# Seven-product units: two of four weight sums made by transfers, the fold in smaller steps, and units in one pair fewer

## The chip, the cores and the metric

The kernel runs on one core of one Trainium2 chip. The metric is the device time of one execution in microseconds, as the median of several runs. A core has a matrix engine (TensorE, in the profile PE, with its weight loads as PEld), a vector engine (VectorE, DVE), an activation engine (ScalarE, ACT), a general engine (GpSimd, POOL) and an engine that here only issues transfers (SyncE, SP). They run side by side and wait for each other by semaphores. Transfers between DRAM and the on-chip memory run on 16 DMA engines; SP, ACT and POOL can issue them.

## The reference

Two layers of an encoder over 256 positions of width 2048 in float32: layer 0 mixes positions by grouped-query attention, layer 1 by dilated windows in three head groups. Each is followed by a gated MLP of width 5632 with a convolution over three positions. The change lies in that MLP's second half, the product with `w_down`:

```
def conv_ffn(h, w_up, conv_w, conv_b, w_down):
    u = h @ w_up                                  # 2048 -> 2 x 5632
    u = conv over 3 positions, per channel, + conv_b
    gate, val = jnp.split(u, 2, axis=-1)
    return (jax.nn.silu(gate) * val) @ w_down     # 5632 -> 2048

for i in range(DEPTH):                            # DEPTH = 2
    h = h + mixer(rms_norm(h, mix_norm[i]), ...)
    h = h + conv_ffn(rms_norm(h, ffn_norm[i]), w_up[i], conv_w[i], conv_b[i], w_down[i])
return rms_norm(h, final_norm)
```

## The kernel before, in words

**Products.** All float32 weights stream once from DRAM in tiles of 128 x 1024 (`raw`, 512 KB: two k-tiles of 128 rows by 512 columns). ACT rounds each into `wh`, DVE makes the rest `wl = raw - wh`, and the 256 positions (two halves m of 128) are kept as `xh`, `xl` in the same way. A product is three matmuls (`xh wh`, `xh wl`, `xl wh`), each 128 x 128 by 512 columns. `feed` (line 103) does this for one group kg of four k-tiles and one block n of 512 columns: two raw tiles, 24 matmuls. There are four raw tiles, two more in the MLP's down stage (`raw_tile`, line 97), and four each of `wh` and `wl`.

**The MLP.** `ffn` (line 368) treats the hidden width in two halves, six and then five pairs p of 512 gate and 512 value columns. Gate and value are evacuated, turned to channel-major by DVE transposes and 16 small copies (`turned`, line 421) into one of three buffers u0 to u2, run through the convolution (`conv`, line 405: four ACT operations, then eight on DVE), multiplied, and split again (`act_split`) to be the left side of the down product. The buffers go round: in a first half the last value uses u0, in a last half the last gate uses u0 and the last value u1. The last value's convolution (`flush`, line 580) runs while the down product has begun.

**Seven-product units.** In three of the four halves (layer 0's first, layer 1's both) the groups kg 2 and 3 go another way. Take the 256 positions as two halves, the four k-tiles as two halves and two blocks of columns n0, n1: that is a product of 2 x 2 blocks, and by a scheme of the Strassen kind it takes seven block products in place of eight, 42 matmuls where two `feed`s need 48. The left sides of the seven come from `combined` (line 476). On the right side four weight matrices b11, b12, b21, b22 are read, and four sums of them are formed by DVE in `fast_unit` (line 493): t1 = b11 + b12 (in u0), b12 + b22 (in place), t2 = b11 + (b12 + b22) (in u1), t4 = t2 + b21 (in u2). The products run in the order 1, 2, 3, 5 (t1), 7 (b12 + b22), 6 (t2), 4 (t4). Products 1, 5, 6 and 7 have four banks of their own; 2, 3 and 4 are added into the accumulators of the plain groups. `fold` (line 526) combines the four banks and adds them to h; it is a generator that is stepped beside the matmuls.

**Order.** `pair` (line 552) does two blocks of columns at once, with the groups and units in a written order. In a first half both pairs have units; in layer 1's last half too, and its last block ends in `project_last` (line 153), which finishes the two halves of the positions one after the other so that the first can be normalised and stored early. Generators in `pending` (evacuations, convolutions, splits) and in `beside` (the fold) are advanced by `step` at fixed places of `feed`: twice `pending`, twice `beside` for each. Before each unit `drain` advances them to their end. The order of issue on each engine follows the program's order with splits and sums drawn ahead (`high_priority`) and with buffers as they come free; each engine and each queue then works strictly in that order.

Of the kernel before, what the change touches and what calls it, by code (L numbers as in the profile page):

```python
# [13 lines left out]
P = 128  # L14
# [16 lines left out]
def tile_encoder(ctx: ExitStack, tc: tile.TileContext, x, xT, w_a, w_ao, q_gain, k_gain, w_b, w_bo,  # L31
# [70 lines left out]

    def feed(accs, lhs, kg, wap, first, last, by_m=False, pieces=1, mid=None, begun=()):
# [11 lines left out]
        def mms(order):  # L115
            for m, kt in order:
                (wh, wl), j = hls[kt // 2], kt % 2
                xh, xl = lhs[4 * kg + kt][:2]
                st, sp = first and kt == 0 and m not in begun, last and kt == 3
                c = slice(m * P, (m + 1) * P)  # L120
                nc.tensor.matmul(accs[m], xh[:, c], wh[:, j, :], start=st, stop=False)  # L121
                nc.tensor.matmul(accs[m], xh[:, c], wl[:, j, :], start=False, stop=False)  # L122
                nc.tensor.matmul(accs[m], xl[:, c], wh[:, j, :], start=False, stop=sp)  # L123
# [29 lines left out]
    def project_last(w, n, lhs, kgs, first_done, last_done):  # L153
# [16 lines left out]
        def mms(o, m, cols, kg, hls, first, last):  # L170
            for kt in range(4):
                (wh, wl), j = hls[kt // 2], kt % 2
                xh, xl = lhs[4 * kg + kt][:2]
                c = slice(m * P, (m + 1) * P)
                nc.tensor.matmul(o, xh[:, c], wh[:, j, cols], start=first and kt == 0, stop=False)
                nc.tensor.matmul(o, xh[:, c], wl[:, j, cols], start=False, stop=False)
                nc.tensor.matmul(o, xl[:, c], wh[:, j, cols], start=False, stop=last and kt == 3)
# [190 lines left out]
    def ffn(l, hT, ss_in, cw, g_next, last, side=None):  # L368
        with tc.tile_pool(name=nm("fpool"), bufs=1) as fp:
# [51 lines left out]
            def turned(s, u, by_act=0):  # L421
# [54 lines left out]
            def combined(cv, k0):  # L476
# [14 lines left out]
                return pick  # L491

            def fast_unit(acc, pick, wap0, wap1, begun, end):
                def load(wap, i):
                    r = raw_tile()
# [3 lines left out]
                def new_sum(i, x, y):  # L499
                    t = u_tile(i)[:, :1024].rearrange("p (a c) -> p a c", a=2)  # L500
                    nc.vector.tensor_tensor(t, x, y, ALU.add)  # L501
                    return t

                b11, b12, b21, b22 = load(wap0, 0), load(wap1, 0), load(wap0, 1), load(wap1, 1)
                with tc.high_priority(offset=2 * AHEAD):
                    t1 = new_sum(0, b11, b12)
                    nc.vector.tensor_tensor(b12, b12, b22, ALU.add)
                    t2 = new_sum(1, b11, b12)
                    t4 = new_sum(2, t2, b21)
                for i, (q, r) in enumerate(((1, b11), (2, b21), (3, b22), (5, t1), (7, b12), (6, t2), (4, t4))):  # L510
                    wh = spool.tile([P, 2, 512], F32R, tag="wh", name=nm("wh"), bufs=NHL)
                    wl = spool.tile([P, 2, 512], F32R, tag="wl", name=nm("wl"), bufs=NHL)
                    with tc.high_priority(offset=AHEAD):
                        nc.scalar.activation(wh, r, AF.Copy)  # L514
# [11 lines left out]
            def fold(acc, n0, n1):  # L526
# [13 lines left out]
                tt(hs(0, n0), hs(0, n0), a, ALU.add)  # L540
                tt(hs(0, n1), hs(0, n1), c, ALU.add)
                yield
                tt(hs(1, n0), hs(1, n0), w, ALU.subtract)
                tt(hs(1, n1), hs(1, n1), v, ALU.add)

            def fast_accs():
                (a3, a8), (a2, a4) = new_acc(), new_acc()
                acc = {q: ps_tile() for q in (1, 5, 6, 7)}
                acc.update({2: a2, 3: a3, 4: a4, 8: a8})
                return acc  # L550
# [774 lines left out]
```

## Time and profile before

| | |
|---|---|
| time, median of 3 runs | 2269.99 us (2268.06 to 2270.1) |
| the profiled execution | 2271.44 us, its span 2269.6 us |
| TensorE busy | 2237.2 us (99%), 10017 matmuls |
| VectorE busy | 1728.1 us (76%) |
| ScalarE busy | 1286.3 us (57%) |
| GpSimd busy | 717.4 us (32%) |
| moved by DMA | 439.57 MB, mean 194 GB/s |
| mean granted clock of TensorE | 0.996 |

Busy times are shares of the span of one profiled execution. A matmul's recorded time overlaps the next one's, so its cost is read from how many fit into a stretch. In a row of a group, `out<-in` names tiles, `xN` counts, and the numbers are busy us, mean ns of one, idle time before. A wait is put down to what ended last. Idle time of an engine that does not set the end costs nothing.

### The profile page before, as it was taken

What the parts mean: (1) busy time and instruction counts of PE and PEld (TensorE: products, weight loads), DVE (VectorE), ACT (ScalarE), POOL (GpSimd) and SP (SyncE); (2) the same over time, 40 slices, a digit from 0 to 9 for tenths busy, and PEclk for the clock granted to TensorE, in tenths of its full rate; (3) what the DMA queues carried; (4) which work ended last, traced back from release to release, by engine and by line L of the source; (5) the groups of instructions that cost most, each with busy time, mean ns of one, the idle gap of its engine ahead of it and who ended that gap; (6) DMA issues with size and microseconds to landing.
All of it is one profiled execution on the core that took longest, in us unless ns stands there. A gap on an engine that the chain in (4) does not pass through costs nothing.

```text
span 2269.6 us, 28639 instructions
## 1 busy us (share of the span) xinstructions
PE 2237.2 (99%) x10017; PEld 1848.8 (81%) x10017; DVE 1728.1 (76%) x2292; ACT 1286.3 (57%) x1791; POOL 717.4 (32%) x939
## 2 busy tenths in 40 slices
PE   9999999999999999999999999999999999999988
PEld 7888888887788888888888888888888878888866
DVE  6877867778866776878877886676768797677797
ACT  7575556556545656555454554445656655555654
POOL 3342065670005552010061007004656300365501
PEclk9999999999999999999999999999999999999999
DMA  8665655554565555565556545566655456555643
GB/s 302 194 219 181 214 195 192 195 194 163 202 205 192 192 195 193 177 206 195 190 187 189 191 168 186 182 202 200 204 194 192 171 204 202 192 194 193 199 169 132
DMA packets 126049, 439.57 MB, mean 194 GB/s; under 512 B 14280, under 2 KB 18120, under 8 KB 125904
## 3 DMA queue, kind: packets, MB, share of 16 engines
q1 hardware_dynamic: 123056, 429.05, 56.5%
q0 software_dynamic: 2560, 8.39, 1.6%
q8 instruction: 78, 1.28, 0.2%
q14 instruction: 67, 0.55, 0.1%
q10 hardware_dynamic: 288, 0.30, 0.0%
HBM read 432.34 MB, written 5.34 MB: 193 GB/s over the span
## 4 chain that ended last, share of the span: by engine, by line
PE 87%; DVE 5%; DMA 2%; POOL 2%; issue 2%; ACT 1%; SPq 0%; DVEq 0%; POOLq 0%; ACTq 0%
PE acc L122 27%; PE acc L121 27%; PE acc L123 27%; DMA raw<-in_w_down_dram 2%; POOL wide L269 2%; DVE wl L515 1%; DVE wl L134 1%; DVE u L501 1%; DMA raw<-in_w_a_dram 1%; PE ps L522 0%; PE ps L521 0%; PE ps L520 0%; PE ps L231 0%; DVE cv L416 0%; PE ps L230 0%
## 5 line engine op out<-in xcount | busy, mean ns | idle before, releaser
L134 DVE TENSOR_TENSOR wl<-raw,wh 128x1024 fp32r<-128x1024 f32 (+1 forms) x756 | 939.7, 1250 | 393.3 <-ACT wh L133 389.0
L133 ACT ACTIVATE wh<-raw 128x1024 fp32r<-128x1024 f32 (+1 forms) x756 | 790.5, 1050 | 680.7 <-PE acc L123 604.0
L121 PE MATMUL acc<-wh,xh 128*128 128x512 f32 x2176 | 848.3, 390 | 0.1
L122 PE MATMUL acc<-wl,xh 128*128 128x512 f32 x2176 | 847.4, 389 | 0.4 <-DVE wl L134 0.2
L123 PE MATMUL acc<-wh,xh 128*128 128x512 f32 x2176 | 847.2, 389 | 0.0
L429 POOL COPY u<-quad 32x256 f32<-32x256 f32 x640 | 457.3, 715 | 331.5 <-DVE quad L265 306.3
L123 PEld LDWEIGHTS acc<-wh,xh 128*128 128x128 f32 x2176 | 408.4, 188 | 85.1
L122 PEld LDWEIGHTS acc<-wl,xh 128*128 128x128 f32 x2176 | 408.7, 188 | 84.8 <-DVE wl L134 2.2
L121 PEld LDWEIGHTS acc<-wh,xh 128*128 128x128 f32 x2176 | 408.7, 188 | 84.0 <-ACT wh L133 0.5
L121 PE MATMUL acc<-wh,a 128*128 128x512 f32 x816 | 319.0, 393 | 7.2 <-DVE h L337 3.7
L122 PE MATMUL acc<-wl,a 128*128 128x512 f32 x816 | 319.9, 392 | 3.1 <-DVE wl L134 3.0
L123 PE MATMUL acc<-wh,a 128*128 128x512 f32 x816 | 319.2, 391 | 0.0
L121 PEld LDWEIGHTS acc<-wh,a 128*128 128x128 f32 x816 | 154.6, 189 | 40.6 <-ACT wh L133 4.5
L122 PEld LDWEIGHTS acc<-wl,a 128*128 128x128 f32 x816 | 154.2, 189 | 36.5 <-DVE wl L134 4.8
L123 PEld LDWEIGHTS acc<-wh,a 128*128 128x128 f32 x816 | 154.1, 189 | 32.3 <-DVE a L216 0.2
L269 POOL COPY wide<-quad 32x256 f32<-32x256 f32 x165 | 107.2, 650 | 171.8 <-DVE quad L265 162.7
L399 POOL MEMSET u<- 128x4 f32 x12 | 1.0, 106 | 421.0 <-DVE wl L515 233.3
L365 ACT ACTIVATE stg<-acc,rstd 128x512 f32<-128x512 f32 x122 | 82.7, 684 | 32.3 <-PE acc L123 32.3
L446 POOL TENSOR_TENSOR cv<-cg,cv 128x1024 f32<-128x1024 f32 x18 | 57.9, 3215 | 108.3 <-DVE cv L416 108.3
L416 DVE SCALAR_TENSOR_TENSOR cg<-u,cw,cg 128x256 f32<-128x256 f32 x176 | 81.7, 507 | 4.5 <-ACT cg L408 4.5
L514 ACT ACTIVATE wh<-raw 128x1024 fp32r<-128x1024 f32 x48 | 50.6, 1058 | 56.2 <-PE acc L123 47.2
L416 DVE SCALAR_TENSOR_TENSOR cv<-u,cw,cv 128x256 f32<-128x256 f32 x176 | 73.9, 477 | 2.9 <-ACT cv L408 2.8
(220 smaller groups left out, 1738.5 us busy)
## 6 DMA issues: line engine op xcount, KB each, us to landing
raw<-in_w_up_dram SPq DMA_DIRECT2D x352, 512.0 KB, 4.5
raw<-in_w_down_dram SPq DMA_DIRECT2D x176, 512.0 KB, 4.5
raw<-in_w_b_dram SPq DMA_DIRECT2D x144, 512.0 KB, 4.4
raw<-in_w_bo_dram SPq DMA_DIRECT2D x48, 512.0 KB, 3.7
raw<-in_w_a_dram SPq DMA_DIRECT2D x40, 512.0 KB, 4.7
raw<-in_w_ao_dram SPq DMA_DIRECT2D x32, 512.0 KB, 4.3
raw<-in_w_a_dram SPq DMA_DIRECT2D x16, 256.0 KB, 5.8
there<-quad POOLq DMA_DIRECT2D x6, 512.0 KB, 3.3
```

The source lines that it names most:

```text
L121: nc.tensor.matmul(accs[m], xh[:, c], wh[:, j, :], start=st, stop=False)
L122: nc.tensor.matmul(accs[m], xh[:, c], wl[:, j, :], start=False, stop=False)
L123: nc.tensor.matmul(accs[m], xl[:, c], wh[:, j, :], start=False, stop=sp)
L133: nc.scalar.activation(wh[:, c], r[:, c], AF.Copy)
L134: nc.vector.tensor_tensor(wl[:, c], r[:, c], wh[:, c].bitcast(F32), ALU.subtract)
L269: nc.gpsimd.tensor_copy(o[32 * c:32 * c + 32, :, 32 * q:32 * q + 32], quad[32 * q:32 * q + 32, c])
L365: nc.scalar.activation(o[:, m, :], accs[m], AF.Copy, scale=rstd[:, m:m + 1])
L416: nc.vector.scalar_tensor_tensor(cj, halves(flat[:, j, o:o + NT])[:, ::-1], tap(n, j, i), cj, ALU.mult, ALU.add)
L429: nc.gpsimd.tensor_copy(o, src)
L446: made.append(eng.tensor_tensor(cv, cg, cv, ALU.mult).ins)
L501: nc.vector.tensor_tensor(t, x, y, ALU.add)
L514: nc.scalar.activation(wh, r, AF.Copy)
```

## The change

In `fast_unit` two of the four sums are no longer made by DVE. t1 and t3 = b12 + b22 are made by loading the first matrix and then adding the second by an accumulating transfer that GpSimd issues; t1 goes into u0 and t3 into a raw tile. t2 = t1 + b22 and t4 = t2 + b21 stay on DVE and are issued at the product that needs them. A unit issues seven transfers instead of four. `fold` yields after nearly every operation. In `pair` the four extra banks are taken at the first unit, pending work is advanced by two more steps after each plain group in the first pair, and is brought to its end only before the first unit. The 16 copies of the last value alternate between GpSimd and ACT (all on ACT before). In layer 1's last half the second pair has no units: its two blocks are plain (`project`, `project_last`), for which `plain_too` keeps the left sides of groups 2 and 3 in plain form as well; `of_m` picks a half of the positions from either form. There are ten units instead of twelve.

```diff
+    def of_m(x, m):
+        return x[m] if isinstance(x, tuple) else x[:, m * P:(m + 1) * P]
...
-            def turned(s, u, by_act=0):
+            def turned(s, u, by_act=False):
...
-                    if i < 16 - by_act:
+                    if i % 2 == 0 or not by_act:
                         nc.gpsimd.tensor_copy(o, src)
...
-                turned(s, blk[1], 16 if blk[0] - NPAIR in (HALVES[0][1] - 1, NPAIR - 1) else 0)
+                turned(s, blk[1], blk[0] - NPAIR in (HALVES[0][1] - 1, NPAIR - 1))
...
-                    slots[-1 - k0 // 4] = combined(cv, k0)
+                    slots[-1 - k0 // 4], *rest = combined(cv, k0)
+                    if hf == 1:
+                        plain_too(k0, 20 + 2 * fast.index(k0 // 4), *rest)
...
+            def plain_too(k0, spot, v, sx):
+                c = pair_slot(spot, [P, 2, 2, P], F32R, "c")
+                split_in_order(c[:, 0], c[:, 1], v[:, 0, :, 1])
+                for kt in range(4):
+                    b, j = divmod(kt, 2)
+                    one = (sx[:, 4, j], sx[:, 5, j]) if b else (c[:, 0, j], c[:, 1, j])
+                    slots[k0 + kt] = (sx[:, b, j], one[0]), (sx[:, 2 + b, j], one[1])
...
-                b11, b12, b21, b22 = load(wap0, 0), load(wap1, 0), load(wap0, 1), load(wap1, 1)
-                with tc.high_priority(offset=2 * AHEAD):
-                    t1 = new_sum(0, b11, b12)
-                    nc.vector.tensor_tensor(b12, b12, b22, ALU.add)
-                    t2 = new_sum(1, b11, b12)
-                    t4 = new_sum(2, t2, b21)
-                for i, (q, r) in enumerate(((1, b11), (2, b21), (3, b22), (5, t1), (7, b12), (6, t2), (4, t4))):
+                def load_sum(wapx, i, wapy, k, r=None):
+                    r = load(wapx, i, r)
+                    nc.gpsimd.dma_start(r.rearrange("p a c -> p (a c)"), wapy[:, k * 1024:(k + 1) * 1024],
+                                        accum_op=ALU.add)
+                    return r
...
+                t1 = load_sum(wap0, 0, wap1, 0, spot(0))
+                b11 = load(wap0, 0)
+                t3 = load_sum(wap1, 0, wap1, 1)
+                b21, b22 = load(wap0, 1), load(wap1, 1)
+                t2, t4 = spot(1), spot(2)
+                for i, (q, r) in enumerate(((1, b11), (2, b21), (3, b22), (5, t1), (7, t3), (6, t2), (4, t4))):
...
                     with tc.high_priority(offset=AHEAD):
+                        if q == 6:
+                            nc.vector.tensor_tensor(t2, t1, b22, ALU.add)
+                        if q == 4:
+                            nc.vector.tensor_tensor(t4, t2, b21, ALU.add)
                         nc.scalar.activation(wh, r, AF.Copy)
                         nc.vector.tensor_tensor(wl, r, wh.bitcast(F32), ALU.subtract)
...
             def fold(acc, n0, n1):
...
                 nc.scalar.activation(a, acc[1], AF.Copy)
+                yield
                 tt(v, acc[6], a, ALU.subtract)
+                yield
                 tt(w, acc[7], v, ALU.add)
                 yield
...
-            def pair(wd, ns, lhs, order, done):
-                while beside:
-                    step(True)
-                acc, begun = fast_accs(), set()
+            def pair(wd, ns, lhs, order, done, hurry=False):
+                (a3, a8), (a2, a4) = new_acc(), new_acc()
+                acc, begun = {2: a2, 3: a3, 4: a4, 8: a8}, set()
...
-                    if side is None or kg == order[-1][0]:
-                        drain()
...
                     if side is None:
+                        if kg == fasts[0]:
+                            while pending or beside:
+                                step(True)
+                                if pending:
+                                    step()
+                            acc.update({q: ps_tile() for q in (1, 5, 6, 7)})
...
+                    for _ in range(2 * hurry):
+                        if pending:
+                            step()
                     if end:
+                        while beside and hf == 1:
+                            step(True)
                         done(sides[side], ns[side])
...
-                    pair(wd, (0, 1), slots, both[0] + both[1] + f0 + both[4] + f1 + both[5], done)
-                    pair(wd, (2, 3), slots, both[0] + f0 + both[1] + f1 + both[4] + both[5], done)
+                    for ns in (0, 1), (2, 3):
+                        pair(wd, ns, slots, both[0] + both[1] + f0 + both[4] + f1 + both[5], done, ns[0] == 0)
                     continue
-                pair(wd, (0, 1), slots, both[0] + [(1, 0)] + f0 + [(1, 1)] + f1 + both[4], done)
-                acc = pair(wd, (2, 3), slots, [(0, 0)] + f0 + [(1, 0)] + f1 + [(4, 0)], done)
-                while beside:
-                    step(True)
-                hs = h[:, 0, 1536:]
-                nc.vector.tensor_tensor(hs, acc[3], hs, ALU.add)
-                project_last(wd, 3, slots, rest, first_out, last_out)
+                pair(wd, (0, 1), slots, both[0] + [(1, 0)] + f0 + [(1, 1)] + f1 + both[4], done, True)
+                done(project(wd, 2, slots, list(range(np_))), 2)
+                project_last(wd, 3, slots, list(range(np_)), first_out, last_out)
```

More of the change, by code (lines that the diff above doesn't have):

```diff
@@ L119, in mms @@
                 st, sp = first and kt == 0 and m not in begun, last and kt == 3
[L120 to L123, printed above, removed]
+                xh, xl = of_m(xh, m), of_m(xl, m)
+                nc.tensor.matmul(accs[m], xh, wh[:, j, :], start=st, stop=False)
+                nc.tensor.matmul(accs[m], xh, wl[:, j, :], start=False, stop=False)
+                nc.tensor.matmul(accs[m], xl, wh[:, j, :], start=False, stop=sp)
         hls = []
@@ L173, in mms @@
                 xh, xl = lhs[4 * kg + kt][:2]
[L174 to L177, printed above, removed]
+                xh, xl = of_m(xh, m), of_m(xl, m)
+                nc.tensor.matmul(o, xh, wh[:, j, cols], start=first and kt == 0, stop=False)
+                nc.tensor.matmul(o, xh, wl[:, j, cols], start=False, stop=False)
+                nc.tensor.matmul(o, xl, wh[:, j, cols], start=False, stop=last and kt == 3)
         for i, (kg, hls) in enumerate(tail):
@@ L490, in combined @@
                     pick[q] = own[0][:, i], own[1][:, i]
-                return pick
+                return pick, v, sx
+            def plain_too(k0, spot, v, sx):
[5 more added lines that the diff above has]
+                    slots[k0 + kt] = (sx[:, b, j], one[0]), (sx[:, 2 + b, j], one[1])
@@ L493, in fast_unit, with load @@
             def fast_unit(acc, pick, wap0, wap1, begun, end):
-                def load(wap, i):
-                    r = raw_tile()
+                def load(wap, i, r=None):
+                    r = r or raw_tile()
                     nc.sync.dma_start(r.rearrange("p a c -> p (a c)"), wap[:, i * 1024:(i + 1) * 1024])
                     return r
[L499 to L502, printed above, removed]
```

13 lines of the change are left out of this document (6 added, 7 removed).

## The prediction

> **What bounds the kernel now.** I read the page's head first, then busy time by stretch, then the chain of waits on TensorE, then the timeline around the first seven-product unit. The head:
>
> ```profile
> span 2269.6 us, 28639 instructions
> PE 2237.2 (99%) x10017; PEld 1848.8 (81%) x10017; DVE 1728.1 (76%) x2292; ACT 1286.3 (57%) x1791; POOL 717.4 (32%) x939
> ```
>
> TensorE is busy 99% of the span, so only two things can move the time: matmuls added or taken away, and the gaps between them. The gaps lie in few places. Busy time by stretch (stretch, width, then busy us and count for PE, PEld, DVE, ACT, POOL, then granted clock, DMA share, GB/s); a plain stretch first, then the three places with units (A: first layer's first half; B: second layer's first half; C1 and C2: first and second pair of the last half):
>
> ```profile
> 2000.00:2100.00 100.00, 100.00 (x443) 82.81 (x442) 72.48 (x97) 59.83 (x77) 55.64 (x72) 1.00 0.58 192
> 540.00:600.00 60.00, 54.61 (x228) 43.12 (x227) 54.89 (x59) 27.90 (x31) 0.00 (x0) 0.97 0.54 184
> 1815.00:1865.00 50.00, 45.03 (x192) 35.47 (x192) 47.00 (x50) 26.79 (x29) 0.00 (x0) 1.00 0.61 209
> 2155.00:2185.00 30.00, 24.16 (x94) 18.15 (x93) 29.41 (x36) 17.93 (x26) 0.00 (x0) 0.94 0.42 143
> 2185.00:2230.00 45.00, 40.80 (x166) 32.42 (x165) 39.80 (x41) 23.92 (x28) 7.32 (x4) 0.92 0.49 167
> ```
>
> The plain stretch gives the price of a matmul: 100/443 = 0.226 us. TensorE's idle time (width less busy) is 5.4 in A, 5.0 in B, 5.8 in C1, 4.2 in C2. After a gap the granted clock falls, which costs about (1 - clock) x width: 1.8 in A, 0 in B, 1.8 in C1, 3.6 in C2. Losses: A 7.2, B 5.0, C1 7.6, C2 7.8, together **27.6 us**. That is all this change can win. DVE is 91 to 98% busy in A, B and C1 against 72% in the plain stretch. The waits on TensorE say the same:
>
> ```profile
> PE ps L521 <- DVE wl L515: 4.7, 4, 1.8
> PE acc L121 <- DVE h L337: 3.7, 2, 2.0
> PE ps L520 <- ACT wh L514: 3.6, 3, 2.3
> PE acc L121 <- DVE h L625: 3.5, 1, 3.5
> PE acc L122 <- DVE wl L134: 3.2, 4, 1.5
> PE acc L520 <- ACT wh L514: 1.2, 2, 0.6
> ```
>
> Lines 514 and 515 are the splits inside a unit; 337 and 625 are the residual adds between the two pairs (A, B; and C), which came late because DVE was at sums and folds. So DVE holds up TensorE here, directly or by sums that ACT waits for.
>
> **The change part by part.** DVE's and ACT's rows (count | busy, mean ns of one | idle before):
>
> ```profile
> L501 DVE TENSOR_TENSOR u<-raw,raw 128x1024 f32<-128x1024 f32 x24 | 29.3, 1221 | 7.8 <-DMA raw<-in_w_down_dram 7.6
> L507 DVE TENSOR_TENSOR raw<-raw,raw 128x1024 f32<-128x1024 f32 x12 | 14.7, 1222 | 2.7 <-DMA raw<-in_w_down_dram 2.7
> L501 DVE TENSOR_TENSOR u<-u,raw 128x1024 f32<-128x1024 f32 x12 | 14.6, 1218 | 0.0
> L515 DVE TENSOR_TENSOR wl<-raw,wh 128x1024 fp32r<-128x1024 f32 x48 | 58.1, 1220 | 9.9 <-ACT wh L514 9.9
> L514 ACT ACTIVATE wh<-u 128x1024 fp32r<-128x1024 f32 x36 | 38.1, 1060 | 34.0 <-DVE u L501 16.7 <-PE acc L123 13.9 <-PE acc L522 2.7
> L429 POOL COPY u<-quad 32x256 f32<-32x256 f32 x640 | 457.3, 715 | 331.5 <-DVE quad L265 306.3
> L431 ACT ACTIVATE u<-quad 32x256 f32<-32x256 f32 x64 | 26.8, 419 | 0.8
> ```
>
> *Sums.* There are 48 sums over 12 units, four each. A unit now costs DVE 4 + 7 operations x 1.22 = 13.4 us; with two sums left it costs 9 x 1.22 = 11.0. Its 42 matmuls, at the unit's own rate (541.48 to 545.67 is 18 of them, 0.233 each, rows below), take 9.8. DVE's debt per unit thus falls from 3.6 to 1.2 us. A plain group of weights lets DVE catch up: its 24 matmuls take 5.4 us and need two splits, 2.4 us.
>
> *Last half, second pair (C2).* Two units become plain work: 12 matmuls more, 12 x 0.226 = 2.7 us lost. In return no sum and no fold stands ahead of the residual add at line 625, and the new accumulators can take the pair of banks that is freed a group earlier. All 7.8 us should go, as plain stretches have no gap. Net gain **5.1**. The extra split for plain use of the two groups (one ACT and one DVE operation on 256 elements each, under half of 1.06 and 1.22 us) lies beside a plain group, where both engines have room; without that cover at most 2 x (0.53 + 0.61) = 2.3 us are lost.
>
> *Accumulating transfers.* The waits that this adds: SyncE's load of the first sum's base waits for buffer u0, which the convolution still reads; loads queued behind it wait too. POOL's accumulate then waits for that landing. Behind it on POOL stand only the second accumulate, and in C the multiplications by the final gain (7.32 us in C2's row), which nobody needs before the end. Transfers as the trace shows them (KB each, median us from issue to landing):
>
> ```profile
> raw<-in_w_down_dram SPq DMA_DIRECT2D x176, 512.0 KB, 4.5
> there<-quad POOLq DMA_DIRECT2D x6, 512.0 KB, 3.3
> oc<-in_onehot_dram POOLq DMA_DIRECT2D x1, 512.0 KB, 7.4
> ```
>
> No accumulate is in the trace. The lower bound is POOL's 512 KB store, 3.3; POOL's 512 KB load of 7.4 is the nearest row, the same size, queue and direction, so I take 7.4; it excludes nothing above, and I keep 14.8, twice it, as the upper end. A first sum is then ready for TensorE 4.5 + 7.4 + 1.06 (its ACT split) = 13.0 us after u0 is free.
>
> The Trainium skill ("Collectives: The Full Stack", section "The bandwidth ceiling: the fold count and why AG ≠ RS ≠ AR") says that an add in flight needs two source reads on the same read ring, so it moves at half the rate. No run here shows it. Only the moving part would double: an estimate from the row below, 0.524 MB at 345 GB/s, adds 1.5 us to each landing, and my sum would end at 2259 instead of 2256.
>
> Where does 13.0 us fit? Timelines of A and C (start, us, operation):
>
> ```profile
> 521.57 1.71 ACT L431 ACTIVATE u<-quad 32x256 f32<-32x256 f32 x4
> 540.26 1.40 DVE L416 SCALAR_TENSOR_TENSOR cv<-u,cw,cv 128x256 f32<-128x256 f32 x3
> 542.71 1.22 DVE L501 TENSOR_TENSOR u<-raw,raw 128x1024 f32<-128x1024 f32 x1
> 541.48 0.40 PE L520 MATMUL ps<-wh,sx 128*128 128x512 f32 x1
> 545.67 0.39 PE L520 MATMUL ps<-wh,s 128*128 128x512 f32 x1
> 547.39 0.50 PE L521 MATMUL ps<-wl,s 128*128 128x512 f32 x1 [1.34 <-DVE wl L515]
> ...
> 2144.66 0.48 DVE L416 SCALAR_TENSOR_TENSOR cg<-u,cw,cg 128x256 f32<-128x256 f32 x1
> 2164.01 1.40 DVE L416 SCALAR_TENSOR_TENSOR cv<-u,cw,cv 128x256 f32<-128x256 f32 x3
> 2165.44 1.23 DVE L501 TENSOR_TENSOR u<-raw,raw 128x1024 f32<-128x1024 f32 x1
> 2157.75 0.40 PE L520 MATMUL ps<-wh,sx 128*128 128x512 f32 x1
> 2161.94 0.39 PE L520 MATMUL ps<-wh,s 128*128 128x512 f32 x1
> 2167.87 0.50 PE L520 MATMUL ps<-wh,s 128*128 128x512 f32 x1 [2.31 <-ACT wh L514]
> 2170.13 0.50 PE L521 MATMUL ps<-wl,s 128*128 128x512 f32 x1 [1.75 <-DVE wl L515]
> ```
>
> In A, u0 is the last value's buffer: the last convolution ends at 541.66, and the unit's first sum starts right behind it. TensorE reaches the product of that sum (the fourth) at 545.67. The change frees u0 sooner: eight of sixteen copies leave ACT (8 x 0.42 = 3.4 us: 538.3 at the latest), and the steps are issued earlier. The floor is eight POOL copies from 521.57 at 0.72 (527.3) and a convolution that runs its course in some 6 us: 533.3. I take the middle, 535.8. The product is ready at 535.8 + 13.0 = 548.8, so TensorE waits 3.1 us, with 1.8 for the clock as in A now. A's other waits go: DVE has two sums fewer, and the fold no longer comes in a block before the add at 337. A: 7.2 to 4.9, gain **2.3**. B is built the same: 5.0 to 4.9, gain **0.1**. If the copies on POOL were slow and nothing came sooner, 541.66 + 13.0 - 545.67 = 9.0 would be waited, 5.9 more in each.
>
> In C1, u0 is the last gate's buffer, free at 2145.14, so its first product is ready at 2158.1, ahead of 2161.94. What TensorE waits for there now (2.31 and 1.75) is the third sum, whose buffer u1 the last convolution holds until 2165.41; 3.4 earlier is 2162.0, plus sum and split (1.22 + 1.06) 2164.3, when TensorE is at 2161.94 + 12 x 0.233 = 2164.7. The next unit's first sum: 2163.2 + 13.0 = 2176.2, needed at about 2157.75 + 60 x 0.233 + 24 x 0.226 = 2177.2. Both just fit; I leave 1.0 for DVE's debt. C1: 7.6 to 1.0, gain **6.6**. The later units of A and B have a full pair of groups (48 matmuls, 10.8 us) between them, and from one unit's third sum to the next one's fourth product TensorE has 12 x 0.233 + 10.8 + 18 x 0.233 = 17.8 us of work, against 13.0.
>
> *Transfers as a load.* A unit with its two groups reads 11 x 0.524 MB instead of 8 in 20.6 us: 280 GB/s instead of 204.
>
> ```profile
> 570.00:580.00 10.00, 10.00 (x45) 8.20 (x44) 10.00 (x11) 6.84 (x7) 0.00 (x0) 1.00 0.71 245
> ```
>
> Full queues would be 245/0.71 = 345 GB/s, so 280 is 81%. I cost it at nothing: buffers are loaded several groups ahead, and the first matrix's buffer now comes free right after its split. Views by index, the later allotment of four banks and the finer fold do no work of their own; DVE's fold operations stay, under plain groups.
>
> Sum: 2.3 + 0.1 + 6.6 + 5.1 = 14.1. The profiled execution took 2271.44 us (span 2269.6); 2257.3 is left, and the median of the runs stands 1.45 lower: **2256**.
>
> **Rivals.** *All waits go* (u0 at the floor 533.3, accumulates near 3.3): 27.6 - 2.7 = 24.9 gained, 2245. For it: 11.0 against 9.8 us is a small debt. Against it: the 7.4 row.
>
> *DVE still holds the units* (11.0 is above 9.8): A, B and C1 keep their 19.8, only C2's 5.1 is won: 2265. Against it: DVE's catch-up between units is 3.0 us a group.
>
> *Slower: accumulates that land late.* With landing time L, the waits are L - 4.3 in A and in B, L - 8.4 and L - 11.2 in C1's units; with 1.8 of clock at three places, 1.0 and 2.7, gain turns to loss at about L = 11.7. At 14.8 the sum is 40, 13 slower: 2283; and the other four units then lack 4.5 + 14.8 + 1.06 - 17.8 = 2.6 each: 2293. For it: no row of an accumulate, and a queue at 81%. Against it: L must exceed the nearest row by 4.3 us.
>
> **How the numbers follow.** My forecast (2251 to 2264) 0.48; all waits go 0.14; DVE still holds 0.12; late accumulates 0.22; something in between, such as loads stuck on SyncE behind the wait for u0, 0.04. About 0.2% (4.5 us) is what a measurement here tells from no change; half of the DVE case and the last one fall inside: faster 0.69, same 0.09, slower 0.22. The range 2245 to 2283 leaves out a few hundredths below and a tenth above.
>
> **What would show it.** Right: no gap after 2190 before the end; DVE's share in A and B near 80%; line 501's and 507's groups down to two sums a unit; the fourth product's split (ACT, from u0) waiting some 3 us for a POOL-issued transfer in A and B, not in C; that transfer landing near 7 us. Wrong: landings above 11 us, a DMA share near 0.9, waits of TensorE at plain loads behind a unit, or waits at the add on line 337's counterpart.

## The result, and the profile after

The changed kernel takes 2274.02 us (median of 20 runs, 2267.52 to 2282.83); the kernel before, run beside it, 2270.17 us. The ratio is 1.0018, with a 95% interval of 1.0009 to 1.0027: so some 4 us were lost where 14 were to be won. The profiled execution of the changed kernel took 2274.03 us with a span of 2272.2 us. Its head:

```profile
span 2272.2 us, 28705 instructions
PE 2241.3 (99%) x10029; PEld 1852.9 (82%) x10029; DVE 1688.0 (74%) x2251; ACT 1266.0 (56%) x1754; POOL 756.2 (33%) x991
```

There are the 12 more matmuls, and DVE is relieved of 40 us, as the change intends. The time is not shorter all the same. Busy time by stretch of the kernel after, with the two second pairs of the first halves added (600 to 640 and 1865 to 1915; columns as in the prediction):

```profile
540.00:600.00 60.00, 55.28 (x233) 44.32 (x232) 43.61 (x47) 28.69 (x30) 4.35 (x5) 0.97 0.79 240
600.00:640.00 40.00, 36.60 (x160) 29.42 (x159) 23.53 (x21) 18.87 (x19) 1.73 (x2) 1.00 0.74 211
1815.00:1865.00 50.00, 44.13 (x174) 34.53 (x173) 33.90 (x35) 22.97 (x23) 3.46 (x4) 0.90 0.77 218
1865.00:1915.00 50.00, 48.75 (x214) 39.61 (x213) 32.68 (x31) 23.68 (x23) 2.58 (x3) 1.00 0.76 233
2155.00:2185.00 30.00, 28.03 (x120) 21.88 (x119) 25.74 (x32) 20.50 (x30) 9.00 (x12) 1.00 0.78 215
2185.00:2230.00 45.00, 42.84 (x184) 33.83 (x183) 32.03 (x33) 22.72 (x28) 8.54 (x4) 1.00 0.74 233
```

The losses by the prediction's rule (width less busy, and (1 - clock) x width) give this table. Before, TensorE was busy 40.00 of 40 and 50.00 of 50 us in the two second pairs, so nothing was lost there.

| stretch | before | forecast | after |
|---|---|---|---|
| A, 540 to 600 | 7.2 | 4.9 | 4.7 + 1.8 = 6.5 |
| second pair behind A, 600 to 640 | 0 | 0 | 3.4 |
| B, 1815 to 1865 | 5.0 | 4.9 | 5.9 + 5.0 = 10.9 |
| second pair behind B, 1865 to 1915 | 0 | 0 | 1.25 |
| C1, 2155 to 2185 | 7.6 | 1.0 | 2.0 |
| C2, 2185 to 2230 | 7.8 | 0 | 2.2 |
| 12 more matmuls | - | 2.7 | 2.7 |
| sum | 27.6 | 13.5 | 28.9 |

So the last half came within 3.2 us of its forecast, and the two first halves, 12 us above theirs, took it all back. The waits on TensorE, after (engine, line waited for, us in total, times, longest):

```profile
PE ps L541 <- DVE wl L535: 9.0, 8, 2.8
PE ps L540 <- ACT wh L534: 5.8, 2, 3.4
PE acc L541 <- DVE wl L535: 3.3, 4, 1.5
```

The waits at the residual adds, 3.7 and 3.5 us before, are gone. What is left is at the splits inside the units (lines 534 and 535). Yet DVE, which makes those splits, was 91 and 94% busy in A and B before and is 73 and 68% busy now. It is late while it has time to spare. Its groups say why (count | busy, mean ns of one | idle time before them, and what ended it):

```profile
L531 DVE TENSOR_TENSOR u<-u,raw 128x1024 f32<-128x1024 f32 x10 | 12.3, 1226 | 56.8 <-DMA u<-in_w_down_dram 31.4 <-DMA raw<-in_w_down_dram 25.4
```

Line 531 is the third sum, t2 = t1 + b22. DVE stood still 56.8 us in front of its ten executions. In six of them (31.4 us) the accumulate that completes t1 (`u`) landed last; in the other four (25.4 us) it was the plain load of b22 (`raw`), the last of a unit's loads on SyncE. The timeline around the second unit of A shows what stands behind it. First DVE (start, us, operation, idle before), then TensorE at the unit's first two products, then the transfers issued from 545 to 570 (KB each, us from issue to landing) and the issue of the two that matter:

```profile
567.32 1.23 DVE L531 TENSOR_TENSOR u<-u,raw 128x1024 f32<-128x1024 f32 x1 [6.31 <-DMA u<-in_w_down_dram]
568.46 1.22 DVE L535 TENSOR_TENSOR wl<-raw,wh 128x1024 fp32r<-128x1024 f32 x1
569.60 1.22 DVE L533 TENSOR_TENSOR u<-u,raw 128x1024 f32<-128x1024 f32 x1
570.73 2.35 DVE L535 TENSOR_TENSOR wl<-raw,wh 128x1024 fp32r<-128x1024 f32 x2
...
568.39 0.40 PE L540 MATMUL ps<-wh,sx 128*128 128x512 f32 x1
569.73 0.50 PE L541 MATMUL ps<-wl,sx 128*128 128x512 f32 x1 [0.94 <-DVE wl L535]
572.00 0.50 PE L541 MATMUL acc<-wl,sx 128*128 128x512 f32 x1 [0.60 <-DVE wl L535]
...
u<-in_w_down_dram SPq DMA_DIRECT2D x1, 512.0 KB, 6.6
u<-in_w_down_dram POOLq DMA_DIRECT2D x1, 512.0 KB, 9.4
...
550.69 0.33 SPq L509 DMA_DIRECT2D u<-in_w_down_dram  x1
557.87 0.86 POOL L514 DMA_DIRECT2D u<-in_w_down_dram  x1 [14.23 <-DMA raw<-in_w_down_dram]
```

The unit's seven products are ordered so that the two sums made by transfers are wanted only at the fourth and fifth. But line 531, drawn ahead by its priority, stands in DVE's queue in front of the split (568.46) of the first product, which needs no sum at all. The base load is issued at 550.69, when u0 comes free, and lands 6.6 us later; the accumulate is issued at 557.87 (its row names a load beside it as the one that it waited for last) and lands 9.4 us later, at 567.3; only then may DVE go on. ACT had split the first matrix long before (560.43 to 561.49 on its timeline), so TensorE starts at 568.39 and stops at the second matmul.

### The profile page after: what moved, and what is told of

It reads as the page before. It is cut to its first block, busy times and chain, and to the rows that moved or that the text cites. A ratio compares the mean times of both kernels' runs of the same rounds, so it can differ in the third digit from the quotient of the medians.

```text
span 2272.2 us, 28705 instructions
## 1 busy us (share of the span) xinstructions
PE 2241.3 (99%) x10029; PEld 1852.9 (82%) x10029; DVE 1688.0 (74%) x2251; ACT 1266.0 (56%) x1754; POOL 756.2 (33%) x991
## 3 DMA queue, kind: packets, MB, share of 16 engines
q1 hardware_dynamic: 124496, 434.30, 58.2%
## 4 chain that ended last, share of the span: by engine, by line
PE 89%; DMA 4%; DVE 3%; POOL 2%; issue 1%; ACT 1%; SPq 0%; DVEq 0%; POOLq 0%; ACTq 0%
PE acc L125 28%; PE acc L124 28%; PE acc L126 28%; DMA u<-in_w_down_dram 2%; POOL wide L272 2%; DMA raw<-in_w_down_dram 1%; DVE wl L535 1%; DVE wl L137 1%; DMA raw<-in_w_a_dram 1%; PE ps L541 1%; PE ps L542 0%; PE acc L541 0%; PE ps L540 0%; ACT wh L136 0%; PE acc L542 0%
## 5 line engine op out<-in xcount | busy, mean ns | idle before, releaser
L137 DVE TENSOR_TENSOR wl<-raw,wh 128x1024 fp32r<-128x1024 f32 (+1 forms) x764 | 952.3, 1252 | 396.0 <-ACT wh L136 391.2
L136 ACT ACTIVATE wh<-raw 128x1024 fp32r<-128x1024 f32 (+1 forms) x764 | 799.5, 1050 | 707.0 <-PE acc L126 629.0
L432 POOL COPY u<-quad 32x256 f32<-32x256 f32 x672 | 477.3, 710 | 340.2 <-DVE quad L268 313.8
L534 ACT ACTIVATE wh<-raw 128x1024 fp32r<-128x1024 f32 x40 | 42.2, 1058 | 51.7 <-PE acc L126 23.5
```

The lines of the kernel that those rows point to most:

```text
L136: nc.scalar.activation(wh[:, c], r[:, c], AF.Copy)
L137: nc.vector.tensor_tensor(wl[:, c], r[:, c], wh[:, c].bitcast(F32), ALU.subtract)
L432: nc.gpsimd.tensor_copy(o, src)
```

## The experiments

The kernel before was run beside each group of four; the ratios are to it. Theory 1 was, at first, that the place of the sum t2 in DVE's queue takes the gain; theory 2 that the accumulates themselves are late or dear. From e9 on, the numbers of the theories belong to the single expectation.

**e1: each sum behind the split of the product before it.** `rest` is the DVE split of the last product.

```diff
                         if q == 6:
-                            nc.vector.tensor_tensor(t2, t1, b22, ALU.add)
+                            with tc.issue_after(rest):
+                                nc.vector.tensor_tensor(t2, t1, b22, ALU.add)
                         if q == 4:
-                            nc.vector.tensor_tensor(t4, t2, b21, ALU.add)
+                            with tc.issue_after(rest):
+                                nc.vector.tensor_tensor(t4, t2, b21, ALU.add)
...
-                        nc.vector.tensor_tensor(wl, r, wh.bitcast(F32), ALU.subtract)
+                        rest = nc.vector.tensor_tensor(wl, r, wh.bitcast(F32), ALU.subtract).ins
```

> One edit on the changed kernel: the third sum t2 (and t4) may stand on DVE only behind the split of the product before it, so it is no longer drawn ahead of the unit's first splits. Theory 1 (DVE's queue stands still behind a sum that waits for an accumulating transfer, and the first splits of the unit behind it are late): the waits at the first products of the later units go (some 5.6 us in the first layer's half, 5.5 in the second layer's, 2.7 in the last half), the wait at the fourth product of the first unit stays: about 2260. Theory 2 (the transfers themselves, queues at a share of 0.77 to 0.79): the waits stay whatever DVE's order, 2271 to 2275.

Measured: 2299.28 us, ratio 1.0122 (1.0108 to 1.0136), 25 us slower than the kernel after. Both theories missed it. Its waits:

```profile
PE ps L543 <- ACT wh L537: 9.6, 10, 2.4
PE ps L544 <- DVE wl L538: 8.4, 13, 0.8
PE acc L543 <- ACT wh L537: 8.0, 10, 0.9
```

The waits stand ten times or a little more, once in every unit: a split on DVE, then the sum, then its ACT split, then its DVE split, one behind the other. In its timeline the sum starts at 575.72 and the split of its result on DVE at 578.14, with 1.21 us idle between. Putting an operation as late as it can go leaves nothing to cover its own successors. So "behind" was right and "right behind" wrong.

**e2: t1 into a buffer that comes free sooner.** Before and after, t1 goes into u0, which in a first half the last convolution still reads when the first unit is near.

```diff
-                t1 = load_sum(wap0, 0, wap1, 0, spot(0))
+                at = (1, 2, 0) if hf == 0 else (2, 0, 1)
+                t1 = load_sum(wap0, 0, wap1, 0, spot(at[0]))
...
-                t2, t4 = spot(1), spot(2)
+                t2, t4 = spot(at[1]), spot(at[2])
```

> One edit on the changed kernel: t1 goes into the buffer that is free first (u1 in a first half, u2 in a last half) instead of u0, so that its load need not wait for the last convolution. Theory 1: the accumulate lands earlier, but the third sum is then drawn ahead of even the first unit's splits; little is won, 2268 to 2278. Theory 3 (the wait for u0 is what costs): the waits at the first unit's fourth product go, 5.2 us in the first layer and 6.6 in the second: about 2263.

Measured: 2269.35 us, ratio 0.9993 (0.9984 to 1.0002), 5 us better than after and in theory 1's range. The wait of the first units at the fourth product is gone, but the others grew:

```profile
PE ps L542 <- DVE wl L536: 14.0, 8, 4.5
```

At the second unit of A (DVE's row, and the accumulate's landing between 540 and 570):

```profile
565.02 1.23 DVE L532 TENSOR_TENSOR u<-u,raw 128x1024 f32<-128x1024 f32 x1 [8.74 <-DMA u<-in_w_down_dram]
u<-in_w_down_dram POOLq DMA_DIRECT2D x1, 512.0 KB, 11.8
```

t1's buffer is free at 546.2, 4.5 us sooner than in after, but TensorE, no longer held at the first unit, comes 5.8 us sooner too (562.59), and the accumulate now takes 11.8 us where it took 9.4. DVE stands still 8.74 us with the first splits behind it. One wait was traded for the other.

**e3: e1 and e2 together.** The diff is both.

> Both edits on the changed kernel: t1 in the buffer that is free first, and the sums behind the split of the product before. Theories 1 and 3 together: both kinds of waits go, 13.8 and some 11 us: about 2250. Theory 2: 2268 or more.

Measured: 2289.05 us, ratio 1.0079 (1.0066 to 1.0092). The new buffers make it 10 us better than e1, but it is far from the 2250 of theories 1 and 3: e1's chain stays (8.9 us in 11 waits for ACT's splits).

**e4: all four sums back on DVE, everything else of the change kept.** The two sums at the products 6 and 4 go.

```diff
-                t1 = load_sum(wap0, 0, wap1, 0, spot(0))
-                b11 = load(wap0, 0)
-                t3 = load_sum(wap1, 0, wap1, 1)
-                b21, b22 = load(wap0, 1), load(wap1, 1)
-                t2, t4 = spot(1), spot(2)
+                b11, t3, b21, b22 = load(wap0, 0), load(wap1, 0), load(wap0, 1), load(wap1, 1)
+                t1, t2, t4 = spot(0), spot(1), spot(2)
+                with tc.high_priority(offset=2 * AHEAD):
+                    nc.vector.tensor_tensor(t1, b11, t3, ALU.add)
+                    nc.vector.tensor_tensor(t3, t3, b22, ALU.add)
+                    nc.vector.tensor_tensor(t2, b11, t3, ALU.add)
+                    nc.vector.tensor_tensor(t4, t2, b21, ALU.add)
```

> The changed kernel with all four sums on DVE again, from four plain loads, as before; fold, steps, copies and the plain last pair stay changed. Theory 1: what the other edits win shows (5.1 us in the last pair, 3.7 and 1.8 at the residual adds between pairs), and DVE's debt at the first units stays: about 2260, so the accumulating transfers cost 14 us net. If the accumulating transfers help on the whole: above 2275.

Measured: 2256.18 us, ratio 0.9939 (0.9925 to 0.9952). This is the forecast's time, reached without the accumulating transfers that the forecast was about. Their part of the change, with the place that it gives t2 and t4, costs 1.0018 - 0.9939 = 0.79%, 18 us. Busy time by stretch in A and B of e4:

```profile
540.00:600.00 60.00, 59.71 (x261) 48.30 (x260) 53.19 (x55) 31.19 (x30) 0.00 (x0) 1.00 0.63 210
1815.00:1865.00 50.00, 49.82 (x219) 40.76 (x219) 41.22 (x42) 23.88 (x24) 0.00 (x0) 1.00 0.60 200
```

TensorE loses 0.3 and 0.2 us there, with DVE 89 and 82% busy and four sums in every unit. One wait of 1.3 us is left behind B, at 1877.56, and one in C1 that e9 looks at. So DVE can be that busy without holding TensorE up.

**e5: t2 and t4 behind the split of the third product.** This is the middle between after and e1: out of the first splits' way, with work left between the sum and the product that reads it. `made[q]` is the DVE split of product q.

```diff
                         if q == 6:
-                            nc.vector.tensor_tensor(t2, t1, b22, ALU.add)
+                            with tc.issue_after(made[3]):
+                                nc.vector.tensor_tensor(t2, t1, b22, ALU.add)
```

(and the same for t4).

> One edit on the changed kernel: t2 and t4 may stand on DVE only behind the split of the unit's third product, so neither ahead of the first splits nor (as in the run before) one by one between the last splits. Theory 1 (DVE's queue blocked by the early sum): the waits at the first products of the later units go, 13.8 us, and no chain of sum and split takes their place; the wait at the first units' fourth product stays: about 2260. Theory 2 (the transfers): 2271 to 2277.

Measured: 2267.18 us, ratio 0.9984 (0.9975 to 0.9993), 7 us better than after and between the two theories. The sum's group:

```profile
L533 DVE TENSOR_TENSOR u<-u,raw 128x1024 f32<-128x1024 f32 x10 | 12.2, 1221 | 14.1 <-DMA u<-in_w_down_dram 14.1
```

DVE stands still 14.1 us for it instead of 56.8, and at the first products TensorE waits no more. What stays, some 14 us in all, is the first units' wait for u0 (2.5 us the longest) and some 1 us a unit at the fourth product, where the two sums now stand in a row ahead of its split (570.83 and 572.09 in the second unit of A).

**e6: e5 and e2 together**, sums behind the third split and t1 in the buffer that is free sooner.

> The edit of the run before and t1 in the buffer that is free first. Theories 1 and 3: the first units' wait goes too, 5.2 and 6.6 us: about 2249, below the version with all sums on DVE (2256). If the transfers hold the units back as well: 2256 or more.

Measured: 2256.79 us, ratio 0.9933 (0.9919 to 0.9946). This is the time that the expectation gave for transfers that still hold the units back, not the 2249 of theories 1 and 3. DVE's idle time before t2 is 3.5 us in all, one wait for an accumulate in C1. TensorE still waits 7.1 us in seven places for DVE's splits, the longest of 2.0 us, at 2174.98, behind that one. So with queue and buffer mended the change as a whole wins 0.7%, but its accumulates win nothing over e4, whose DVE makes twice as many sums; and e9 below, which gives e4 the new buffers (and draws the last half's sums less far ahead), is 8 us faster than e6.

**e7: the addition left out of the transfers.** The same transfers in the same places, but without `accum_op`, so the second matrix overwrites the first and t1 and t3 are not sums.

> The changed kernel with the accumulating transfers as plain ones of the same size, issued by GpSimd at the same places with the same waits; left out of the computation is the addition (t1 and t3 are their second matrix alone). If the add in flight doubles a read and so delays the landing: from GpSimd's issue to landing falls from 8.8 us to 7.4 or less, and the time to 2265 to 2270. If the landing is that of GpSimd's queue under load: 8 us or more, and 2271 to 2277.

Measured: 2258.35 us, ratio 0.9939 (0.9927 to 0.9952), faster than either theory gave. So adding in flight alone costs 16 us here. t2 still stands in its bad place, and DVE still idles 42.4 us before it, but TensorE waits 8.5 us at the units' splits where it waited 18.9. The transfers from POOL, first after, then e7 (KB each, median us from issue to landing), and the queue they use (packets, MB, share of 16 engines' span), for both, with the plain queue of after:

```profile
raw<-in_w_down_dram POOLq DMA_DIRECT2D x10, 512.0 KB, 8.8
u<-in_w_down_dram POOLq DMA_DIRECT2D x10, 512.0 KB, 8.8
q1 hardware_dynamic: 124496, 434.30, 58.2%
q0 software_dynamic: 5440, 18.88, 4.2%
```

```profile
raw<-in_w_down_dram POOLq DMA_DIRECT2D x10, 512.0 KB, 6.7
u<-in_w_down_dram POOLq DMA_DIRECT2D x10, 512.0 KB, 7.3
q0 software_dynamic: 5440, 18.88, 3.0%
```

The landing is 1.5 to 2.1 us longer with the addition, as the first theory had it. For the same packets and bytes the queue takes 4.2% x 16 x 2272.2 = 1527 us of engine time against 3.0% x 16 x 2256.6 = 1083. The 444 us more, over 20 transfers of 512 KB in packets of 4 KB (2560), are 173 ns a packet (within 14, as the shares are rounded); a plain packet of q1 takes 58.2% x 16 x 2272.2 / 124496 = 170 ns. An accumulating packet costs about two plain ones.

That makes it a load on all other transfers too. These are the ten us in which the second unit of A is loaded and begins, first after, then e7 (columns as above):

```profile
560.00:570.00 10.00, 9.06 (x40) 7.22 (x39) 3.69 (x4) 4.25 (x4) 0.86 (x1) 1.00 0.97 254
560.00:570.00 10.00, 9.39 (x41) 7.35 (x41) 5.19 (x5) 4.68 (x6) 0.00 (x0) 1.00 0.71 282
```

With the addition the DMA engines are full (0.97) at 254 GB/s; without it 282 GB/s take a share of 0.71. How late an accumulate lands goes with that share. In after, t1's accumulate in the first units of A and B took 5.5 and 5.4 us, with shares of 0.52 and 0.58 between its issue and its landing (542.74 to 548.24, 1818.07 to 1823.45); those issued at 557.87 and 622.59 took 9.4 and 11.6, with 0.96 and 0.99.

**e8: the kernel before with only the second pair of the last half made plain** (`plain_too`, `of_m` and the two plain blocks; no accumulates, old fold, order and copies).

```diff
-                acc = pair(wd, (2, 3), slots, [(0, 0)] + f0 + [(1, 0)] + f1 + [(4, 0)], done)
...
-                project_last(wd, 3, slots, rest, first_out, last_out)
+                done(project(wd, 2, slots, list(range(np_))), 2)
+                project_last(wd, 3, slots, list(range(np_)), first_out, last_out)
```

> The kernel before with one part of the change alone: the last half's second pair without units. By the prediction's term for it 7.8 us of gaps go and 2.7 us of matmuls come: 5.1 us faster, 2266. Rival: the first pair's fold and residual adds now collide with the plain blocks, and nothing is won: 2271.

Measured: 2268.43 us, ratio 0.9993 (0.9984 to 1.0001).

```profile
2155.00:2185.00 30.00, 23.40 (x89) 17.70 (x88) 28.39 (x36) 17.55 (x25) 0.00 (x0) 0.89 0.33 114
2185.00:2230.00 45.00, 45.00 (x198) 36.84 (x198) 33.43 (x34) 24.28 (x29) 7.52 (x4) 1.00 0.65 226
```

C2 has no gap left, 7.8 us won for 2.7 us of matmuls, as forecast. C1 lost 2.3 us more than before (6.6 + 3.3 = 9.9 against 7.6), as the rival had it in part, which leaves 2.8. The medians differ by 2.4 us, but the interval still holds 1, so the gain itself isn't shown by the times.

**e9: e4 with the sums taken out of the way.** What was left in e4 was above all one wait of 4.29 us (behind it the granted clock was 0.50 from 2166 to 2170):

```profile
2163.74 1.22 DVE L527 TENSOR_TENSOR u<-u,raw 128x1024 f32<-128x1024 f32 x1
2164.87 1.22 DVE L137 TENSOR_TENSOR wl<-raw,wh 128x1024 fp32r<-128x1024 f32 x1
...
2166.15 0.80 PE L125 MATMUL acc<-wl,a 128*128 128x512 f32 x1 [4.29 <-DVE wl L137]
```

Here too sums (lines 524 to 527) stand ahead of a split that TensorE needs sooner, that of a plain group.

```diff
-                t1, t2, t4 = spot(0), spot(1), spot(2)
-                with tc.high_priority(offset=2 * AHEAD):
+                t1, t2, t4 = (spot(i) for i in ((1, 2, 0) if hf == 0 else (2, 0, 1)))
+                with tc.high_priority(offset=(2 - hf) * AHEAD):
```

> All four sums on DVE as in e4, the first sum now written to a buffer that is free before the last convolution ends (u1 in the first half, u2 in the last), and in the last half the sums are drawn ahead by 60 instead of 120 places. Theory 1 (what is left in e4 is the wait of the plain split in the second layer's first pair, 4.45 us at 2166.15 with the slower clock behind it, 2.5, and 2.5 us of first-unit waits, because the sums stand ahead of that split): these go, 2248 to 2252. Theory 2 (DVE's debt is simply moved to the split behind): 2255 or more.

Measured: 2249.01 us, ratio 0.9906 (0.9891 to 0.9921), 21 us faster than before and 25 faster than the change. Which of the two edits, the buffer or the later drawing in the last half, won how much of the 7 us over e4 was not asked. The 4.29 us wait is gone and no wait inside a unit is above 0.7 us:

```profile
PE acc L538 <- ACT wh L532: 0.7, 1, 0.7
```

It is the fastest kernel of this study, and beats both.

**e10, e11, e12: one more part of the change undone in e4 each**, to see which of them won A and B: the fold in four lumps (e10), all sixteen copies of the last value on ACT (e11), the old order of the second pairs (e12).

```diff
 # e11
-                    if i % 2 == 0 or not by_act:
+                    if not by_act:
 # e12
-                        pair(wd, ns, slots, both[0] + both[1] + f0 + both[4] + f1 + both[5], done, ns[0] == 0)
+                        pair(wd, ns, slots, (both[0] + both[1] + f0 + both[4] + f1 + both[5] if ns[0] == 0 else
+                             both[0] + f0 + both[1] + f1 + both[4] + both[5]), done, ns[0] == 0)
```

In e10 `fold` is as in the kernel before.

> e4 with the fold in four lumps as before, everything else of e4 kept. Theory 1 (the fold in single steps carries most of what the kept parts win in the first pairs, about 12 us): 2262 to 2268. Theory 2 (the earlier steps, the alternating copies or the order of the second pair carry it): 2255 to 2259.

> e4 with all sixteen copies of the last value on ACT as before. Theory 1 (sharing the copies with POOL frees u0 up to 3.4 us sooner and so starts the sums sooner): 3 to 7 us slower than e4, 2259 to 2263. Theory 2 (the copies were never late): 2255 to 2258.

> e4 with the second pair of the first halves in its old order (unit, two groups, unit, four groups). Theory 1 (the order of the second pair puts the units where DVE has caught up, and the add of the first pair no longer meets the first unit): waits come back at the second pairs of both first halves, 2 to 4 us each, 2260 to 2264. Theory 2 (the order does nothing): 2255 to 2258.

Measured: e10 2254.59 us, 0.9929 (0.9917 to 0.9942); e11 2261.11 us, 0.9958 (0.9946 to 0.9970); e12 2255.05 us, 0.9927 (0.9915 to 0.9940). Against e4's 0.9939, e10 and e12 are no slower, so the fine fold and the order win nothing by themselves. The copies seem to: 0.0019, some 4 us, when POOL takes half of them, though the intervals of e4 and e11 touch. The trace of e11 bears it out: its first sum in A starts at 540.38, e4's at 535.30, and more waits stand at the units' splits (e4 has 2.9 us in 4 in the first of these rows, none in the second):

```profile
PE ps L539 <- DVE wl L533: 4.3, 6, 1.7
PE acc L539 <- DVE wl L533: 3.6, 5, 1.1
```

Of e4's 14 us the copies hold about 4 and the plain second pair perhaps 2. The other 8 belong to what wasn't undone singly (the two extra steps after each plain group, work brought to its end only before the first unit, the four banks taken later) or to parts that need each other; which of these it is stays open.

## Why the prediction was wrong

The forecast was 2256 us and faster; 2274 us came. By its steps:

- *The bound and the sum to be won.* Right. Gaps were the only thing to win besides 12 matmuls, and e9 won 21 us, with those 12 matmuls in it.
- *Last half, second pair.* Right: no unit, no gap, and no wait at the add on line 625's counterpart. The 2.2 us that the table shows in C2 are the first pair's second unit (waits of 1.46 and 0.61 us at 2190.30 and 2192.57).
- *C1.* Half right: of 7.6 us 1.0 were to stay. 2.0 were lost before 2185, and with the second unit's two waits 4.1 in all. The forecast had that unit's first sum ready at 2176.2, 1 us before its use. Its accumulate was issued at 2179.35, and DVE waited for it until 2187.89 with the third product's split behind: the same failure as in the later units below.
- *The first units of A and B.* The wait for u0 came at the place forecast, 3.1 us with 1.8 of clock behind it. In A it was 2.42 and 0.76 us with 1.8 of clock; in B 3.40 and 0.47, and some 3.5 of the 5.0 of clock (0.92 and 0.73 in the two stretches of 10 us from 1815), so 2.5 more than forecast. That A fits so well is in part luck: u0 came free at 536.9 in place of 535.8 and the base took 5.3 us in place of 4.5, but the accumulate 5.5 in place of 7.4. TensorE, after:

```profile
549.46 0.51 PE L540 MATMUL ps<-wh,s 128*128 128x512 f32 x1 [2.42 <-ACT wh L534]
550.72 0.79 PE L541 MATMUL ps<-wl,s 128*128 128x512 f32 x1 [0.76 <-DVE wl L535]
...
636.59 0.50 PE L541 MATMUL ps<-wl,sx 128*128 128x512 f32 x1 [2.79 <-DVE wl L535]
...
1824.66 0.79 PE L540 MATMUL ps<-wh,s 128*128 128x512 f32 x1 [3.40 <-ACT wh L534]
1846.63 0.50 PE L541 MATMUL ps<-wl,sx 128*128 128x512 f32 x1 [2.00 <-DVE wl L535]
```

- *The later units of A and B: this step failed.* The forecast set 17.8 us of TensorE's work, up to the next unit's fourth product, against a chain of 13.0, so no wait. The rows at 569.73, 572.00, 636.59 and 1846.63 are such waits. With smaller ones and the slower clock the later units lost some 9.7 of the 12 us by which the first halves missed their forecast. Two things were wrong in the step.

  The first is the deadline. The step asked when TensorE reads t1, and not what is queued on DVE behind the sum that reads t1. With t2 in front of the first product's split, in the second unit of A the accumulate has to be there a sum and a split (2.4 us) before TensorE's second matmul at 568.6, so at 566.2: 15.5 us after u0 came free (550.67, the end of DVE's split of t1). Without t2 there, t1 would be wanted only for the split of the fourth product, which TensorE would reach at 568.39 + 18 x 0.233 = 572.6.

  The second is the size. The chain was put at 4.5 + 7.4 = 11.9 us to the landing; it took 550.67 to 567.3 = 16.6, the base 6.6 and the accumulate 9.4. With the forecast's 11.9 us even the bad place would have been harmless; with 16.6 it is 1.1 us late here, and TensorE's gap is 0.94. In the second unit of B it was not t1 that came last but b22's plain load, issued at 1833.16, 11.0 us from issue to landing where the median of such loads is 4.8. DVE's row, and the loads issued from 1833.1 to 1833.3:

```profile
1844.22 1.23 DVE L531 TENSOR_TENSOR u<-u,raw 128x1024 f32<-128x1024 f32 x1 [8.23 <-DMA raw<-in_w_down_dram]
raw<-in_w_down_dram SPq DMA_DIRECT2D x1, 512.0 KB, 11.0
```

  That both place and size count is what e5 (place mended, 7 us better) and e7 (addition left out, 16 us better) show.
- *Transfers as a load: mis-sized.* The forecast found a share of 81% for 280 GB/s and costed it at nothing. Over the whole of A the share was 0.79, but at 240 GB/s, and in the stretches where the later units' sums were loaded it was 0.97 (560 to 570 and 1835 to 1845). The sum counted an accumulate as one transfer; by e7 its packets cost two. An estimate with the two of a unit's and its groups' eleven transfers counted twice is 280 x 13/11 = 331 of the forecast's 345 GB/s, 96%. The loads into u0 from SyncE took 5.9 us (median) where 4.5 was taken, and plain loads from POOL take 6.7 to 7.3 (e7). That was the forecast's 7.4 for the accumulate; the addition itself, which came on top, was not in it. The Trainium skill ("Collectives: The Full Stack", "The bandwidth ceiling: the fold count and why AG ≠ RS ≠ AR") says of the add in a reduce-scatter that it needs two source reads on one ring, which halves the rate. The trace agrees with the half rate, with 173 ns more on packets of 170, and the estimate of 1.5 us a landing made from it was near the 1.5 to 2.1 measured; that the second read is the reason, no run shows.
- *DVE's debt.* Two sums fewer per unit were to be worth the gain in A and B. They won nothing here: e6 with two sums on DVE and e4 with four take 2256.8 and 2256.2 us. The stretches of before, 91 and 94% busy, were read as an engine at its limit; in e4 it is 89% busy in A and TensorE loses 0.3 us. e11, with the same sums and splits on DVE as e4, waits more because its first sum starts later. So when the sums can start and what they stand in front of matters beside their number; which of the kept parts freed A and B in e4 is open but for the copies.

Of the signs of a wrong forecast that were listed, two came, though not where means and medians are read: two of the twenty accumulates took over 11 us (the one of 11.6 ends in the wait of 2.79 us at 636.59), and the DMA share passed 0.9 in the stretches named. No median was above 11, and TensorE waited neither at plain loads nor at the add. The rival that the time came nearest to, late accumulates, was given a turning point at a landing of 11.7 us. With t2 where the change puts it the second unit of A turns at 15.5 - 7.2 = 8.3 us (7.2 being from u0 free to the accumulate's issue at 557.87), and 8.8 was the median.

## What to carry to other kernels

When an operation on an in-order engine begins to wait for a transfer, its deadline is no longer that of the one who reads its result but of the first thing queued behind it: look up its place in the queue, and move it behind what is urgent, but not so late that its own successors are bare. An engine that is 90% busy in front of a wait need not be its cause; see whether it stood still, and for whom, before work is taken off it. A sum made by two transfers in series is a long chain that begins when its buffer comes free, so it wants the buffer that is free first. And a new kind of transfer is a load on the plain ones beside it: read the DMA share in stretches as short as the wait, since a mean over 60 us hides full queues.

## What the runs showed that was not expected

An accumulating transfer of 512 KB from POOL landed in 8.8 us (median of 20), a plain one in the same place in 6.7 to 7.3 us, and each of its packets cost some 173 ns more than a plain one's 170. Moving two sums by two or three splits in DVE's queue cost 32 us (e1 against e5, 2299.3 and 2267.2 us) with the same instructions on every engine. With 23 us less work on DVE than e4 (1689.8 against 1713.0 us) e6 was no faster, while moving eight copies of 0.42 us from ACT to POOL in each half was worth about 4 us.
